# Second part of the down projection by seven products, residual additions of three norms by accumulating transfers, and another root and other additions for the last 256 tokens

## Chip, core and metric

The kernel runs on one core of one Trainium2 chip. The metric is the device time of one execution in microseconds (us), as the median of the runs shown; lower is better. TensorE is written PE, VectorE DVE, ScalarE ACT, GpSimd POOL, and SP is the engine whose queue issues most transfers.

## The reference, cut to what matters

One layer on 2048 tokens of 1024 channels in float32. What matters here is its end:

```
x = x + rmsnorm(merged @ w_o, norm_mix_post)        # called x1 below
h = rmsnorm(x, norm_mlp_pre)
f = square(relu(h @ w_up)) @ w_down                 # w_up 1024 x 4096, w_down 4096 x 1024
x = x + rmsnorm(f, norm_mlp_post)
rmsnorm(x, g) = x * rsqrt(mean(x * x) + 1e-6) * g
```

## The kernel before

**Layout.** Channels lie on the 128 partitions and tokens along the free axis. There are two blocks of tokens (`b` = 0, 1) of 1024, each of two halves (`t` = 0, 1) of 512. A tile is 128 x 1024: two rows of 128 channels for 512 tokens. Each operand of a product is split into a high part rounded to fp32r (by ACT, `wh` and `big`) and the rest (by DVE, `wl`, `tr`, `big`); three of the four cross products are formed. One `product` is two halves of twelve matmuls, 24 matmuls of 128x128 by 128x512, all recorded at L268 (`matmuls`).

**Down.** `w_down` is cut into four slabs `s` of 1024 rows. Within a slab the product is done as seven products `i` = 1 to 7 in place of eight (Winograd's scheme over two channel groups and the two halves `t`), for both blocks `b` and both output groups `o`, and summed over the slabs in PSUM. Products 1 and 2 both go into the output cells of `t` = 0 with `o` (tile `c00`); 5, 6, 3, 7 go into the others, and 4 into cells `u`.

**First part of down.** Product 1 is itself done by seven products in place of eight, over the grid of `o`, of two groups of slabs, and of `b` (`LEVEL`, `level_weights`, `level_weight`, `level_loads`, `level_parts`, `level_product`). Sums and differences of weights are formed by `level_weights` while up runs and are kept in DRAM (`level`); those of the tokens are formed by the sinks of `mlp_up`.

**The rest of down.** `jobs` lists products 5, 6, 3, 7 (`SHARED`), for each slab and each `b`, with one weight for both blocks; then 4 and 2 (`ALONE`) for `b` = 0 and after that for `b` = 1. `down_product` runs two products (one for each `o`) for a job. `token_cells` loads and splits the tokens of a job two jobs ahead, `weight_down` the weights, and `last_product` adds the sums up in `c00`, `c01`, `c11`, `u`. The last four jobs (`END`: product 2, `b` = 1) run for `o` = 0 only; their `o` = 1 is done by `at_end`.

**The norms.** `Finish` is the last norm of one `b` and `t`. `steps` squares the four tiles, sums them over the channels on PE (`root_pe`, L563), takes the inverse root on DVE (`root_dve`, 14 small instructions with the split), spreads it to all partitions on PE (L662), and multiplies. `finish` then adds x1, which `fetch` loaded into four more tiles, on DVE, and stores the result from SP's queue. Three of the four norms run this way as background work in `Lane` objects: each call of `bg()`, one for each product, takes a number of steps of each lane. The fourth, of `b` = 1 and `t` = 0, is split: `first_squares` prepares three tiles, and `at_end` does the fourth tile in two halves of 256 tokens. In `at_end` the sums of squares are at L1902, matmuls on ones that only fill time at L574 (`IDLE` = 7 and 9 of them), the roots at L603 to L610, the spreads at L654, and the multiplications and additions of `times` and `plus` at L124 and L118. At the end come four pairs of a multiplication and an addition on DVE, each with a store of 256 KB.

**What sets the order.** Each engine runs its own list in order. The lists come from a scheduler that takes instructions by priority; `tc.high_priority(offset)` moves work ahead, `behind()` and `ordered` tie background work to the main line, and `InOrder` keeps the traced order in `at_end`. A tile's reuse waits for whoever used its buffer before; the pool `big` has 28 buffers, `tr` 9, `fo` 6, `wh` and `wl` 3 each. `load` issues on SP's queue, `store` on ACT's, `aside` on POOL's.

Of the kernel before, what the change touches and what calls it, by code (L numbers as in the profile page):

```python
# [59 lines left out]
IDLE = (7, 9)  # L60
# [7 lines left out]
def block_kernel(  # L68
# [560 lines left out]

    def spread_dve(y, tmp):  # L630

        n = y.shape[1]
        yh, yl = small("sp", n, F32R), small("sq", n, F32R)
        nc.vector.tensor_copy(yh, y)
        sub(yl, y, f32(yh))
        if tmp is None:
            return yh, yl
        dg = mk(*tmp, F32R)
        for i, part in enumerate((yh, yl)):
            nc.vector.tensor_tensor(  # L640
                dg[:, i * T : (i + 1) * T].rearrange("p (g q) -> p g q", g=G),
                f32(ident).unsqueeze(1).to_broadcast([P, G, P]),
                f32(part).unsqueeze(2).to_broadcast([P, G, P]),
                op=ALU.mult,
            )
        return dg

# [506 lines left out]
    q2 = {}  # L1154
# [220 lines left out]
    def mlp_scale(b, buf):  # L1375

        st = None
        for t in (0, 1):
            sq = Squares(buf)
            for c in range(0, CPS, 2):  # L1380
                x = [mk(*buf) for _ in (0, 1)]
                for i in (0, 1):
                    load(x[i], x1d[b, c + i, t])
                yield 2
                sq.add(x[0], own=True)
                sq.add(x[1], own=True)
# [12 lines left out]
        yield  # L1399
# [266 lines left out]
    lanes.append(conv1)  # L1666
    def faster():
        conv1.rate = 2.8
# [13 lines left out]
    SHARED, ALONE = (5, 6, 3, 7), (4, 2)  # L1682
# [86 lines left out]
    def last_product(i, o, b, ps):  # L1769
# [14 lines left out]
        elif i == 6:  # L1784
            u[k], c01[k] = mk(*BIG), mk(*BIG)
            to(u[k], c00[k])
            mark(add(c01[k], u[k], c11[k]))
        elif i == 3:
            to(c01[k], c01[k])
            fin[b, 1].ready[o] = c01[k]  # L1790
        elif i == 7:
            to(u[k], u[k])
            mark(add(c11[k], c11[k], u[k]))
            fin[b, 1].ready[o + 2] = c11[k]
        elif i == 4:
            to(u[k], u[k])
            fin[b, 0].ready[o + 2] = u[k]
        else:
            to(c00[k], c00[k])
            fin[b, 0].ready[o] = c00[k]  # L1800

    class Finish:


        def __init__(self, b, t):
            self.b, self.t, self.x, self.ready = b, t, {}, {}
            self.order = (0, 1, 2, 3) if t else (2, 3, 0, 1)
# [6 lines left out]
        def finish(self, c):  # L1814
            y, x = self.ready[c], self.x[c]
            mul(two(y), two(y), per_token(self.rb))
            i = add(x, x, y)
            load(out[self.b, c, self.t], x)
            return i

# [5 lines left out]
        def steps(self, lag):  # L1826
            sq = Squares(FO)
            for c in self.order:
                while c not in self.ready:
                    yield 1  # L1830
                self.squares(sq, c)
                yield
            ss = sq.total()
            yield 2
# [6 lines left out]
            for c in self.order:  # L1841
                self.finish(c)
                yield

# [15 lines left out]
    def at_end(f, w, cells):  # L1860
# [3 lines left out]
        y = c00[k]  # L1864
# [46 lines left out]
        def root(h, st):  # L1911
            q = q2[f.b, f.t][:, h * HG : (h + 1) * HG]
            return spread_dve(root_dve(st[:, :HG], q), None)
# [10 lines left out]
        with tc.high_priority(offset=URGENT):  # L1924
# [5 lines left out]
            st = root_psum()  # L1930
            sums(0, before(0) + [sq[:, 0], sq[:, 1]], st, True, True)
            dg = root(0, st)
            slab(1, 1)
            rbs[0] = spread_pe(dg)
# [9 lines left out]
            st = root_psum()  # L1944
            sums(1, before(1), st, True, False)
# [4 lines left out]
            dg = root(1, st)  # L1950
            rbs[1] = spread_pe(dg)
            for n in f.order:
                times(1, n)
                plus(1, n)
# [28 lines left out]
    level = {}  # L1983

    def level_weights():

        for n in (0, 1):
            def get(s, o):
                t = fo()
                load(t, w_down[2 * s + o, 0])  # L1990
                return t

            def kept_as(k, t):
                level[k, n] = dram("level")
                aside(level[k, n], t)

            a21, a22 = get(n, 1), get(n + 2, 1)
            yield 1
            a11 = get(n, 0)
            add(a22, a21, a22)  # L2000
            kept_as(5, a22)
            yield 1
            sub(a21, a11, a21)
            kept_as(7, a21)
            yield
            sub(a11, a22, a11)
            kept_as(6, a11)
            a12 = get(n + 2, 0)
            yield 1
            sub(a12, a12, a11)  # L2010
            kept_as(3, a12)
            yield

    def level_weight(p, n):

        with tc.high_priority(offset=AHEAD):
            t = mk(p_wr, "wr")
            o = {1: 2 * n, 2: 2 * (n + 2), 4: 2 * (n + 2) + 1}.get(p)
            load(t, level[p, n] if o is None else w_down[o, 0])
            return split_w(t)  # L2020

    def level_loads(p, home):

        b, at, k = {
            1: (0, 0, (0, 0)), 2: (0, SLABS, (0, 0)), 3: (1, SLABS, (0, 0)),
            5: (1, 0, "T1"), 6: (1, SLABS, "T2"), 7: (1, SLABS, "T3"), 4: (1, SLABS, "T4"),
        }[p]
        with tc.high_priority(offset=AHEAD):
            los = [mk(*home, F32R) for _ in range(SLABS)]
            for u, lo in enumerate(los):  # L2030
                load(f32(lo), fd[b, u + at, k])
        return los

# [31 lines left out]

    cells = {}
# [13 lines left out]
    then(lambda: lanes.extend([Lane(1, chain_of(level_weights(), scales()))]), octs[1], 1)  # L2080
    got = []
    then(lambda: got.append(level_loads(LEVEL[0], BIG)), octs[-1], 5)
    then(lambda: got.append(level_loads(LEVEL[1], BIG)), octs[-1], 3)
# [4 lines left out]
    w = [level_weight(LEVEL[0], k) for k in (0, 1)]  # L2088
    here, coming = coming[0], coming[1:]
    for n, p in enumerate(LEVEL):  # L2090
        with behind():
            if n + 1 < len(LEVEL):
                following = [level_weight(LEVEL[n + 1], k) for k in (0, 1)]
# [3 lines left out]
            if n + 2 < len(LEVEL):  # L2097
                coming.append(level_loads(LEVEL[n + 2], (BIG, TR, BIG, TR, BIG)[n]))
# [4 lines left out]
    for n, (s, i, b) in enumerate(jobs[:-SLABS]):  # L2103
        if (s, i, b) == (1, 3, 0):
# [4 lines left out]
        if (s, i) == (0, ALONE[0]):  # L2109
            if b == 0:  # L2110
                lanes += [Lane(2, fin[0, 1].steps(2), fin[1, 1].steps(2))]
            else:
                lanes += [Lane(2, fin[0, 0].steps(2)), Lane(2, fin[1, 0].first_squares())]
        if n and (i in ALONE or b == 0 or (s, i) == FILL[:2]):
            w = [weight_down(i, s, o) for o in (0, 1)]
        cells = coming.pop(0)
        while len(coming) < 2 and n + 1 + len(coming) < len(jobs):
            job = jobs[n + 1 + len(coming)]
            with behind() if n < 8 else nullcontext():
                coming.append(token_cells(*job, BIG if n < 4 else TR))  # L2120
        down_product(s, i, b, w, cells)
    end = []
    for n, (s, i, b) in enumerate(END):
# [80 lines left out]
```

## Time and profile before

| | us |
|---|---|
| median of 3 runs (2167.44 to 2172.89) | 2168.49 |
| profiled execution | 2169.2 |
| its span, first to last instruction | 2167.4 |
| PE busy | 2146.1 |
| DVE busy | 1666.4 |
| ACT busy | 1036.4 |
| POOL busy | 32.3 |

A line of the timeline gives start, duration, engine, line of the kernel, operation, output and inputs by tile name, shape and count; in brackets stands the idle time before it and what ended it. A line of the windows gives the busy time of PE, weight loads, DVE, ACT and POOL in a stretch, the granted PE clock, and the transfers' share and GB/s. Durations overlap where an engine is pipelined; the spacing of starts is what an instruction takes.

### The profile page before, as it was taken

The numbers are of one execution on the slowest core, as the hardware profiler recorded it, in microseconds if no ns is written. First come the engines' busy times: TensorE is split into PE (matmuls) and PEld (weight loads), VectorE is DVE, ScalarE is ACT, GpSimd is POOL, SyncE is SP. The second block draws the span as 40 slices with busy tenths as digits, with TensorE's granted clock in tenths as the row PEclk, the third lists the DMA queues.
The fourth block names the chain that finished last, engine by engine and source line by source line (L and its number), as shares of the span: only waits on it lengthen the run. The fifth ranks groups of instructions, "written<-read, shape, count | busy, mean of one in ns | idle before, by whom it ended". The sixth has DMA issues, their size and how long they took to land.

```text
span 2167.4 us, 25192 instructions
## 1 busy us (share of the span) xinstructions
PE 2146.1 (99%) x9630; PEld 1778.2 (82%) x9630; DVE 1666.4 (77%) x1640; ACT 1036.4 (48%) x1083; POOL 32.3 (1%) x69
## 2 busy tenths in 40 slices
PE   9999999999999999999999999999999999999998
PEld 7888888888888878888888878888888888888887
DVE  8897789998688998987758785777776656546786
ACT  6444454334543535545644674655653332334551
POOL 1000000000000000000000000000000000000000
PEclk9999999999999999999999999999999999999999
DMA  7688997778997787445777698677788996555882
GB/s 276 238 300 311 325 348 279 262 251 294 336 373 252 251 318 278 181 146 194 266 288 279 241 361 320 237 258 272 298 352 305 372 341 232 174 193 186 276 300 86
DMA packets 165416, 587.97 MB, mean 271 GB/s; under 512 B 18352, under 2 KB 20656, under 8 KB 165296
## 3 DMA queue, kind: packets, MB, share of 16 engines
q1 hardware_dynamic: 145168, 513.91, 66.0%
q10 hardware_dynamic: 12672, 46.14, 5.5%
q0 software_dynamic: 7456, 26.31, 3.1%
q8 instruction: 75, 1.23, 0.2%
q14 instruction: 45, 0.37, 0.0%
HBM read 389.07 MB, written 197.23 MB: 271 GB/s over the span
## 4 chain that ended last, share of the span: by engine, by line
PE 92%; DVE 3%; DMA 2%; ACT 1%; issue 1%; SPq 0%; DVEq 0%; ACTq 0%
PE up L268 28%; PE down L268 24%; PE wo L268 7%; PE ga L268 7%; PE glu L268 5%; PE gb L268 5%; PE B L268 4%; PE rb L268 4%; PE A L268 4%; PE pool L268 3%; DVE big L121 1%; DMA tr<-yd 1%; DMA wl<-kept 1%; PE rb L563 1%; PE mix L268 1%
## 5 line engine op out<-in xcount | busy, mean ns | idle before, releaser
L268 PE MATMUL up<-big,wh 128*128 128x512 f32 x1792 | 480.9, 390 | 2.1 <-DVE big L121 1.8
L268 PEld LDWEIGHTS up<-big,wh 128*128 128x128 f32 x1792 | 335.9, 188 | 73.8 <-DVE big L121 2.9
L225 ACT CAST wh<-wr 128x1024 fp32r<-128x1024 f32 x199 | 209.0, 1051 | 375.1 <-PE up L268 91.1
L939 DVE SCALAR_TENSOR_TENSOR y<-v,cst,y 128x1024 f32<-128x1024 f32 x240 | 307.5, 1281 | 2.8
L268 PE MATMUL down<-big,wh 128*128 128x512 f32 x856 | 296.4, 390 | 0.0
L268 PE MATMUL up<-big,wl 128*128 128x512 f32 x896 | 276.2, 389 | 0.0
L225 ACT CAST wh<-ws 128x1024 fp32r<-128x1024 f32 x128 | 134.5, 1052 | 253.6 <-PE up L268 63.6
L268 PE MATMUL down<-big,wl 128*128 128x512 f32 x704 | 216.9, 389 | 0.0
L268 PE MATMUL down<-tr,wh 128*128 128x512 f32 x552 | 214.9, 389 | 0.0
L268 PEld LDWEIGHTS up<-big,wl 128*128 128x128 f32 x896 | 168.2, 188 | 34.8
L121 DVE TENSOR_TENSOR wl<-ws,wh 128x1024 fp32r<-128x1024 f32 x120 | 146.5, 1222 | 64.8 <-ACT wh L225 63.4
L268 PEld LDWEIGHTS down<-big,wh 128*128 128x128 f32 x856 | 160.7, 188 | 33.4
L121 DVE TENSOR_TENSOR wl<-wr,wh 128x1024 fp32r<-128x1024 f32 x122 | 148.7, 1220 | 45.8 <-ACT wh L225 44.7
L121 DVE TENSOR_TENSOR tr<-tr,big 128x1024 fp32r<-128x1024 f32 x92 | 110.5, 1222 | 73.8 <-ACT big L1748 64.2
L268 PEld LDWEIGHTS down<-big,wl 128*128 128x128 f32 x704 | 132.2, 188 | 27.4
L1748 ACT CAST big<-tr 128x1024 fp32r<-128x1024 f32 x82 | 84.4, 1050 | 112.2 <-DMA tr<-fd 96.2
L121 DVE TENSOR_TENSOR big<-big,big 128x1024 fp32r<-128x1024 f32 (+1 forms) x90 | 108.0, 1221 | 30.3 <-ACT big L1748 11.8
L268 PE MATMUL wo<-big,wh 128*128 128x512 f32 x480 | 128.6, 390 | 0.4 <-ACT tr L1312 0.4
L268 PE MATMUL glu<-big,wh 128*128 128x512 f32 x464 | 125.2, 391 | 1.3 <-ACT wh L225 0.9
L268 PEld LDWEIGHTS down<-tr,wh 128*128 128x128 f32 x552 | 103.6, 188 | 21.4
L268 PE MATMUL gb<-big,wh 128*128 128x512 f32 x448 | 120.0, 390 | 0.0
L268 PE MATMUL ga<-big,wh 128*128 128x512 f32 x448 | 119.9, 389 | 0.0
(212 smaller groups left out, 3356.3 us busy)
## 6 DMA issues: line engine op xcount, KB each, us to landing
tr<-fd SPq DMA_DIRECT2D x96, 512.0 KB, 5.3
wr<-w_down SPq DMA_DIRECT2D x90, 512.0 KB, 5.8
wl<-kept SPq DMA_DIRECT2D x85, 512.0 KB, 5.0
kept<-wl SPq DMA_DIRECT2D x72, 512.0 KB, 5.9
wr<-w_up SPq DMA_DIRECT2D x64, 512.0 KB, 4.8
wr<-w_in SPq DMA_DIRECT2D x60, 512.0 KB, 5.4
fd<-tr ACTq DMA_DIRECT2D x54, 512.0 KB, 3.8
fd<-tr SPq DMA_DIRECT2D x46, 512.0 KB, 3.1
```

The source lines that it names most:

```text
L121: return nc.vector.tensor_tensor(o, a, b, op=ALU.subtract)
L225: nc.scalar.copy(hi[:, :n], src[:, :n])
L268: i = nc.tensor.matmul(ps, w[wp][:, (at + k) * P : (at + k + 1) * P], rhs[k][xp], start=start and n == 0, stop=stop and n == len(order) - ...
L563: nc.tensor.matmul(st[:, at + g : at + g + 1], ss[:, g * P : (g + 1) * P], inv_n, start=start is None or (start and g == 0), stop=stop, sk ...
L939: nc.vector.scalar_tensor_tensor(acc, v[:, k : k + TB], wk, acc, op0=ALU.mult, op1=ALU.add)
L1748: nc.scalar.copy(hi, t)
```

## The change

1. **Product 2 by seven products.** `ALONE` becomes `(4,)`. Product 2 runs as `HALVES`, seven products of two halves (48 matmuls each), for both blocks at once, after `SHARED` and before product 4. The first half's weights' sums (`level_weights(2, 0)`) are formed during up of block 0, the second's during products 3 and 7. The new `level_cells` forms the sums of the tokens (16 loads, 16 subtractions, 16 stores) there too. Each `level_half` adds its sum into `c00` on DVE.
2. **Three norms.** `Finish.steps` no longer loads x1: POOL issues a transfer that adds x1 to the scaled tile, and after four of these four stores. The norms of `t` = 1 start with the halves, that of `b` = 0, `t` = 0 with product 4.
3. **The last 256 tokens.** `root_short` takes eight small instructions; the block's epsilon times its factor (`floors`) is added to the sum of squares by a matmul, and the root is spread in plain float32 without a split (`spread_whole`). `IDLE` becomes (7, 5). Two of the four last additions go to POOL; the other two read products written to PSUM, and the very last store is halved over two queues.

The diff, cut to its core:

```diff
-IDLE = (7, 9)
+IDLE = (7, 5)
...
+    def root_short(a, scale):
...
+        y = sm("sy", I32)
+        nc.vector.tensor_scalar(y, a.bitcast(I32), -0.5, MAGIC, op0=ALU.mult, op1=ALU.add)
+        y = f32(y)
+        h = sm("s1")
+        mul(h, y, y)
+        h2 = sm("s2")
+        mul(h2, h, a)
+        h = step(ALU.add, h2, -10.0 / 3.0, h2, "s1")
+        y = step(ALU.add, h, 5.0, y, "sy")
+        h = sm("s1")
+        mul(h, y, y)
+        h = step(ALU.mult, h, -0.5 * 0.375**3 * scale, a, "s2")
+        return step(ALU.add, h, 1.5 * 0.375 * scale, y, "sy")
...
+    def spread_whole(y):
+
+        rb = mk(ps_rb, "rb", F32, (P, T))
+        for g in range(y.shape[1]):
+            nc.tensor.matmul(
+                rb[:, g * P : (g + 1) * P], y[:, g : g + 1].to_broadcast([P, P]), f32(ident),
+                start=g == 0, stop=True, skip_group_check=True,
+            )
+        return rb
...
+        if b:
+            f = floors[b] = p_const.tile([P, G], F32, tag="floor", name="floor")
+            nc.vector.tensor_scalar(
+                f, st[:, :G], EPS, EPS**0.5 * SQ, op0=ALU.add, op1=ALU.mult
+            )
+            mul(f, f, f)
...
+    lanes.append(Lane(1, when_idle(level_weights(2, 0, window, lambda: mk(p_y, "y")), 42)))
...
-    SHARED, ALONE = (5, 6, 3, 7), (4, 2)
+    SHARED, ALONE = (5, 6, 3, 7), (4,)
...
             dg = spread_dve(root_dve(st, q2[self.b, self.t]), FO)
-            self.fetch(self.order)
             yield lag
             self.rb = spread_pe(dg)
             yield 1
             for c in self.order:
-                self.finish(c)
+                y = self.ready[c]
+                mul(two(y), two(y), per_token(self.rb))
+                nc.gpsimd.dma_start(y, x1d[self.b, c, self.t], accum_op=ALU.add)
                 yield
+            for c in self.order:
+                aside(out[self.b, c, self.t], self.ready[c])
+            yield
...
+            rbs[1] = spread_whole(root(st))
+            for n in f.order[:2]:
+                times(1, n)
+                x = at(f.x[n], 1)
+                nc.gpsimd.tensor_tensor(x, x, at(f.ready[n], 1), op=ALU.add)
+                load(two(out[f.b, n, f.t])[:, :, HT:], x)
+            scaled = {}
+            for k, n in enumerate(f.order[2:]):
+                scaled[n] = ps[:, k * T : (k + 1) * T].rearrange("p (c t) -> p c t", c=2)
+                mul(
+                    scaled[n], at(f.ready[n], 1),
+                    rbs[1][:, :HT].unsqueeze(1).to_broadcast([P, 2, HT]),
+                )
+            n = f.order[2]
+            x = at(f.x[n], 1)
+            add(x, x, scaled[n])
+            load(two(out[f.b, n, f.t])[:, :, HT:], x)
+            for i, queue in enumerate((store, load)):
+                x = at(f.x[c], 1)[:, i]
+                add(x, x, scaled[c][:, i])
+                queue(two(out[f.b, c, f.t])[:, i, HT:], x)
...
+                if k == 22:
+                    t = mk(*(BIG if u % 2 else FO))
+                    sub(t, here[22], here[12])
+                    kept_as("V3", u + SLABS, t)
+                elif k == 12:
+                    sub(here[12], here[12], here[11])
+                    kept_as("V1", u, here[12])
+                elif k == 11:
+                    sub(here[22], here[22], here[12])
+                    kept_as("V2", u + SLABS, here[22])
+                else:
+                    sub(here[21], here[21], here[22])
+                    kept_as("V4", u + SLABS, here[21])
...
+    def level_half(p, n, w, cells):
+
+        a = {1: "x", 2: "z", 6: "x", 7: "x", 4: "x", 5: "y", 3: "y"}[p]
+        if p in (1, 2, 5) and n == 0:
+            sums_of[a] = psum("down")
+        ps = sums_of[a]
+        product(
+            ps, w, cells, start=p in (1, 2, 5) and n == 0, stop=p in (2, 4, 3) and n == 1
+        )
+        if n:
+            k = {1: (0, 0), 2: (0, 0), 6: (0, 1), 3: (0, 1), 5: (1, 1), 7: (1, 1), 4: (1, 0)}[p]
+            with tc.high_priority(offset=AHEAD):
+                mark(add(c00[k], c00[k], ps))
+            if p in (2, 3, 7, 4):
+                fin[k[1], 0].ready[k[0]] = c00[k]
+        bg()
...
+    HALVES = [(p, n) for p in LEVEL for n in (0, 1)]
+    at = next(n for n, job in enumerate(jobs) if job[1] in ALONE)
+    PREPARE = (0, 3, 0)
+    items = jobs[:at] + HALVES + jobs[at:]
...
+        if item == PREPARE:
+            lanes.append(Lane(1.2, chain_of(level_weights(2, 1, fo), level_cells())))
+        if (s, i, b) == (0, ALONE[0], 0):
+            lanes.append(Lane(3, fin[0, 0].steps(2, 150)))
```

In the code after the change, weights and cells of a half are prepared two halves ahead, and the loads of its cells four ahead.

More of the change, by code (lines that the diff above doesn't have):

```diff
@@ L1812, in fetch @@
                 load(self.x[c], x1d[self.b, c, self.t])
[L1814 to L1819, printed above, removed]
         def squares(self, sq, c):
@@ L1909, in before, with floor, root @@
             return [f.ss[:, h * HT : (h + 1) * HT]]
-        def root(h, st):
-            q = q2[f.b, f.t][:, h * HG : (h + 1) * HG]
-            return spread_dve(root_dve(st[:, :HG], q), None)
+        def floor(h):
+            st = root_psum()
+            nc.tensor.matmul(
+                st[:, :HG], f32(ident), floors[f.b][:, h * HG : (h + 1) * HG],
+                start=True, stop=False, skip_group_check=True,
+            )
+            return st
+        def root(st):
+            return root_short(st[:, :HG], SQ)
         def times(h, c):
@@ L1943, in at_end @@
             plus(0, c)
-            st = root_psum()
-            sums(1, before(1), st, True, False)
+            st = floor(1)
+            sums(1, before(1), st, False, False)
             idle(IDLE[0], first[:, :T])
@@ L1982, in block_kernel, with level_weight @@
     LEVEL = ORDER
[L1983 to L2014, printed above, removed]
+    def level_weight(part, p, n):
         with tc.high_priority(offset=AHEAD):
```

182 lines of the change are left out of this document (137 added, 45 removed).

## The prediction

> **What bounds the kernel now.** I read the page first (busy shares, then the chain that ended last), then the waits of PE, then windows by stage from the end back, then the timeline of the last 80 us. A window starts where a stage's first matmul is, counted back from the end.
>
> ```profile
> PE 2146.1 (99%) x9630; PEld 1778.2 (82%) x9630; DVE 1666.4 (77%) x1640; ACT 1036.4 (48%) x1083; POOL 32.3 (1%) x69
> ...
> PE 92%; DVE 3%; DMA 2%; ACT 1%; issue 1%; SPq 0%; DVEq 0%; ACTq 0%
> ```
>
> PE is busy for 2146 of 2167 us and makes 92% of the chain. A matmul taken away anywhere before the end shortens the run, as long as PE is still fed; the few us in which PE is idle lie in the tail.
>
> ```profile
> core 0: us, PE busy (x) PEld busy (x) DVE busy (x) ACT busy (x) POOL busy (x), PEclk, DMA share, GB/s
> ...
> 1558.00:1636.00 78.00, 78.00 (x346) 64.58 (x345) 57.75 (x50) 43.85 (x45) 0.00 (x0) 1.00 0.85 332
> 1636.00:1723.00 87.00, 87.00 (x385) 72.09 (x384) 54.51 (x47) 31.57 (x32) 2.12 (x4) 1.00 0.94 351
> ...
> 1810.00:1897.00 87.00, 87.00 (x386) 72.06 (x385) 48.76 (x43) 30.61 (x32) 0.00 (x0) 1.00 0.56 193
> 1897.00:1973.00 76.00, 76.00 (x337) 62.96 (x336) 39.77 (x35) 26.73 (x28) 0.00 (x0) 1.00 0.52 178
> ...
> 2104.00:2126.00 22.00, 22.00 (x99) 18.23 (x98) 21.60 (x19) 13.90 (x15) 0.00 (x0) 1.00 0.42 149
> ```
>
> These are the first part of down by seven products (1558), products 5 (1636), 3 (1810) and 7 (1897), and the four END jobs (2104). PE is full in each, also where transfers run at 351 GB/s, and where DVE is busy for 98% of a stretch. So a stage of either kind is not lost by its mean load; it is lost where one input comes late.
>
> **Part 1, the matmuls.** Product 2 was 4 slabs x 2 blocks x 2 outputs = 16 products of 24 matmuls, 384. It becomes 14 halves of 24, 336. The instruction lists of both programs agree: 2368 full matmuls into `down` and its `rb` banks before, 2320 after.
>
> ```profile
> 2094.23 0.84 PE L268 MATMUL down<-big,wl 128*128 128x512 f32 x3
> ...
> 2096.95 0.84 PE L268 MATMUL down<-big,wl 128*128 128x512 f32 x3
> ```
>
> Twelve matmuls lie between these two starts: 2.72 / 12 = 0.2267 us. 48 x 0.2267 = **-10.9 us**, if PE stays fed.
>
> **Its price on DVE.** The lists show 25 more DVE instructions of 128x1024: 16 in `level_cells`, 8 in the second `level_weights`, 12 more splits of cells, 3 more joins; 2 fewer splits of weights and 12 fewer additions of x1.
>
> ```profile
> 2083.23 4.62 DVE L121 TENSOR_TENSOR tr<-tr,big 128x1024 fp32r<-128x1024 f32 x4
> ...
> 2095.07 0.15 DVE L610 SCALAR_TENSOR_TENSOR s<-s 128x4 f32<-128x4 f32 x1
> 2095.26 0.16 DVE L610 SCALAR_TENSOR_TENSOR sy<-s,sy 128x4 f32<-128x4 f32 x1
> ...
> 2096.53 0.68 DVE L640 TENSOR_TENSOR fo<-ident,sp 128x512 fp32r<-128x512 f32 x1
> 2097.13 0.69 DVE L640 TENSOR_TENSOR fo<-ident,sq 128x512 fp32r<-128x512 f32 x1
> ```
>
> Back to back, 128x1024 takes (4.62 - 1.22) / 3 = 1.13 us, 128x512 0.60, a small one 0.20. Products 3 and 7 (163 us, DVE 88.5) get 20 of the new ones, 23 us: 68% busy, hidden behind PE. Their 40 new transfers of 512 KB are 21 MB, 129 GB/s on top of 193 and 178; the stage at 351 shows room for that. Four more run during up of block 0, where the new list puts them after the convolution's work; they too cost nothing. If that cover is gone, each costs 1.1 us.
>
> The halves are the tight place. They last 14 x 24 x 0.2267 = 76.2 us, and the new DVE list holds, from the join before them up to the join that ends them, 58 instructions of 128x1024, 5 of 128x512 and 14 small: 65.5 + 3.0 + 2.8 = 71.3 us, 94%. I walked the list against PE's. It is on time except in two places. In the second half of sub-product 2, a cell's split ends 0.5 us after PE wants it. Then PE wants the spread of the norm of `b` = 0, `t` = 1 eight matmuls into the second half of sub-product 7, 7.3 us after sub-product 5 ends; but DVE has to do the join of sub-product 5, three splits, the last twelve small instructions and the two 128x512 of the spread in between: 4 x 1.13 + 12 x 0.20 + 2 x 0.60 = 8.1, and some 0.3 of handing over: 1.1 us late. With ragged edges I take **+2.0**, from 0 (all handed over early) to 10 (first rival). What waits behind a late split is the whole PE list, so each such wait counts in full.
>
> **Part 2, the norms.** The 12 additions of x1 leave DVE; the multiplications stay. Nothing on PE's path waits for a stored tile except buffers: casts for `at_end`'s weights wait for the stores of the norm `b` = 1, `t` = 1, scaled some 35 us before.
>
> ```profile
> fd<-fo POOLq DMA_DIRECT2D x22, 512.0 KB, 6.6
> big<-x1d SPq DMA_DIRECT2D x16, 512.0 KB, 7.0
> out<-big SPq DMA_DIRECT2D x12, 512.0 KB, 6.0
> ...
> x1d<-big POOLq DMA_DIRECT2D x8, 512.0 KB, 5.6
> ```
>
> No row shows an accumulating transfer. Below it costs a plain one, 5.6; above, a load and a store one after the other, 7.0 + 6.0 = 13.0. I take 8, near the plain rows, then a 6 us store: 14 of the 35. The last norm (`b` = 0, `t` = 0) is scaled while `at_end` runs, and here POOL's two last additions are queued behind its four stores, which wait for its accumulations. Its last multiplication ends about 6.5 us after the first join of `at_end` and POOL's first addition is due about 20 us after that join, so an accumulation has 13 us before it delays anything. Cost at 8: nothing. The Trainium skill, "Collectives: The Full Stack", section "The bandwidth ceiling: the fold count and why AG ≠ RS ≠ AR", speaks against this: an add in the transfer needs two reads, so it runs at about half a copy's rate. By that 6.6 becomes about 13, an estimate, and the slack would be just used up; no run here shows it yet.
>
> ```profile
> 2098.31 0.62 PE L662 MATMUL rb<-fo,ones 128*128 128x512 f32 x2
> ...
> 2138.41 0.39 PE L268 MATMUL down<-big,big 128*128 128x256 f32 x1 [0.78 <-DVE big L118]
> ```
>
> One small gain: PE's list puts this norm's spread (two matmuls, 0.45) into the 0.78 us that PE idles at `at_end`'s first join: **-0.4**.
>
> **Part 3, the tail.**
>
> ```profile
> 2152.01 0.69 DVE L118 TENSOR_TENSOR big<-big,down 128x512 f32<-128x512 f32 x1 [1.15 <-PE down L268]
> 2152.17 1.87 PE L574 MATMUL rb<-ones 128*128 128x512 f32 x7
> ...
> 2154.86 0.16 DVE L124 TENSOR_TENSOR s<-rb,q 128x2 f32<-128x2 f32 x1 [1.56 <-PE rb L1902]
> ...
> 2157.54 0.30 PE L654 MATMUL rb<-ident,sp 128*128 128x128 f32 x1 [0.55 <-DVE sp L634]
> ...
> 2158.24 0.69 DVE L124 TENSOR_TENSOR big<-big,rb 128x512 f32<-128x512 f32 x1 [0.64 <-PE rb L654]
> ...
> 2162.93 0.69 DVE L118 TENSOR_TENSOR big<-big,big 128x512 f32<-128x512 f32 x1
> ```
>
> From the first root instruction to PE's spread are 2.68 us; eight small ones and 0.15 of handing over make 1.75: -0.9. The floor's matmul ahead of the sums adds 0.1. The spread has two float32 matmuls for four in fp32r; before it takes 0.70 (2157.54 to 2158.24), and I take 0.7, from 0.4 (half) to 1.4 (double). DVE's eight instructions spaced 0.67 (2158.24 to 2162.93 is seven) last 5.4 to 2163.6. Now there are four multiplications and one addition of 128x512, 3.35, and two of 128x256, about 0.4 each: 4.15, so -1.2. Four fewer fillers: nothing, they end before the root.
>
> ```profile
> 2.21 0.30 POOL L725 CAST ident<-tr 128x128 fp32r<-128x128 f32 x1
> ...
> 2159.68 4.51 SPq L127 DMA_DIRECT2D out<-big  x4
> ...
> out<-big SPq DMA_DIRECT2D x8, 256.0 KB, 2.4
> ```
>
> POOL's two additions hide if each takes under 1.7. Bounds: 0.69 as on DVE; 2.4, eight times the cast's 0.30 (four times its width, two inputs). I take 1.4; at 2.4 the end is 1.4 later. The Trainium skill, "GPSIMD Engine Reference", section "3.1 Elementwise — side-by-side cycle accounting", has such an addition at 1.96 times DVE's, 1.35 by our row: hidden as well. The last store has half the bytes: from 0 to -0.6, I take -0.2. Tail: -0.9 + 0.1 - 1.2 - 0.2 = **-2.2**.
>
> **Sum.** 2169.2 - 10.9 + 2.0 - 0.4 - 2.2 = 2157.7 against the profiled execution. That one lies 0.7 above the median of 2168.49, so **2157** as a median.
>
> **Rivals.** *PE waits at handovers in the halves.* For it: the cast and the split of a cell follow each other on two engines, each in order.
>
> ```profile
> L121 DVE TENSOR_TENSOR big<-big,big 128x1024 fp32r<-128x1024 f32 (+1 forms) x22 | 26.0, 1220 | 10.3 <-ACT big L1074 8.1 <-ACT big L1748 2.2
> ...
> L121 DVE TENSOR_TENSOR tr<-tr,big 128x1024 fp32r<-128x1024 f32 x8 | 9.4, 1220 | 4.0 <-ACT big L1074 4.0
> ...
> L121 DVE TENSOR_TENSOR tr<-tr,big 128x1024 fp32r<-128x1024 f32 x92 | 110.5, 1222 | 73.8 <-ACT big L1748 64.2 <-PE down L268 5.1 <-ACT big L1074 4.0
> ```
>
> In the first part of down, DVE idles 14.3 us before 30 splits, 0.48 each. With 28 splits that is 13.4 in the halves, where only 4.9 are free: PE is 8.5 late in place of 2.0, **2163.5**. Against it: there PE never waited, so DVE was early; and in the halves casts come two halves ahead. *The same on the slower side:* over the whole kernel the wait is 73.8 / 92 = 0.80 for a split. At that, for 42 splits of cells and weights, 33.6 - 4.9 = 28.7 us late: **2184**. It decides from (4.9 + 2 + 11.5) / 42 = 0.44 us per split of all 42 for no gain, and 0.6 for slower by over 0.3%.
>
> *Accumulations hold up the tail.* Place: POOL's additions behind the four stores. Beyond 13 us each us counts; at 20 us it is **2164**. Against it: the plain rows.
>
> That the change doesn't take the matmuls away is excluded by the lists.
>
> **How the numbers follow.** About 0.3% (6.5 us) is what a measurement can tell from no change: faster is below 2162.0, slower above 2175.0. Forecast (2153 to 2161): 0.62. First rival at 2161 to 2168: 0.18; its slower form: 0.08. Accumulations late, 2158 to 2172: 0.09, half of it below 2162. Better than 2153: 0.03. Faster: 0.62 + 0.03 + 0.05 + 0.05 of the first rival's edge = 0.75; slower 0.08; same 0.17. The range begins at 2153 (no wait, -2.0; the best ends of the spread and the store, -0.3 and -0.4; and 1 us, by which the fastest run of before lies under its median) and ends at 2166, past the first rival.
>
> **What would show it.** In the changed profile: 48 fewer L268 matmuls into `down`; PE's busy share of the halves (76 us before product 4) near full, with waits of 1 to 3 us on a DVE split or the spread; the landing of the accumulating transfers under 13 us; the last root in eight instructions; DVE's last addition some 9.5 us after the last join's start, 11.6 before. Wrong would be PE idle for over 5 us in the halves, or POOL's additions starting late.

## The result, and the profile after

| | before | after |
|---|---|---|
| median of 12 runs, run in turns | 2171.03 | 2163.52 |
| lowest and highest | 2166.32, 2172.89 | 2161.95, 2173.23 |
| ratio of after to before, 95% interval | | 0.9978 (0.9969 to 0.9987) |
| profiled execution | 2169.2 | 2163.6 |
| its span | 2167.4 | 2161.7 |

By the ratio of the runs the change makes the kernel faster by 0.22% (0.13 to 0.31), some 5 us; the medians lie 7.5 us apart, the means 4.6 (2170.2 and 2165.5). That is below the 0.3% that the prediction called measurable; the twelve runs in turns resolve a little more. The forecast of 11.5 us was more than twice the gain by the ratio. 2163.5 lies inside the range of 2153 to 2166, near the first rival's 2163.5, but not by that rival's mechanism: that is luck. Six of the twelve runs of the changed kernel had a mean granted clock of 0.997 or 0.998 and took 2162.0 to 2163.4 us, the other six 0.994 or 0.995 and 2163.6 to 2173.2; the profiled one, at 0.995, is of the second kind, so the slow clock that its trace shows below need not be in every run.

The page of the changed kernel, the lines that answer to those of before:

```profile
PE 2139.8 (99%) x9582; PEld 1772.0 (82%) x9582; DVE 1688.4 (78%) x1654; ACT 1044.3 (48%) x1093; POOL 78.0 (4%) x143
...
PE 88%; DVE 5%; DMA 4%; issue 1%; ACT 1%; SPq 0%; DVEq 0%; ACTq 0%
```

PE has its 48 matmuls fewer, but is busy for 6.3 us less, not 10.9, and its share of the chain fell from 92% to 88%. DVE and transfers took the difference: somewhere PE waited. All waits of PE after 1900 us (engine, line, tile waited for; sum, times, longest):

```profile
PE rb L563 <- DVE fo L118: 2.4, 1, 2.4
PE down L268 <- DVE tr L121: 0.5, 1, 0.5
PE rb L678 <- DVE sy L639: 0.4, 1, 0.4
PE down L268 <- DVE big L118: 0.3, 1, 0.3
PE rb L698 <- DVE fo L666: 0.2, 1, 0.2
```

The two that were predicted are there: 0.5 at a split in sub-product 2 and 0.2 at the spread (1.1 predicted). The largest was not predicted: 2.4 us at the sum of squares of the norm `b` = 1, `t` = 1. PE asks for it at 2063, in product 4, 15 us behind the end of the halves (they run from 1969 to 2048). Windows of the changed kernel around it:

```profile
2020.00:2040.00 20.00, 19.79 (x88) 16.03 (x87) 19.10 (x24) 17.30 (x22) 4.69 (x6) 1.00 1.01 316
2040.00:2060.00 20.00, 20.00 (x90) 16.57 (x89) 17.31 (x16) 15.48 (x18) 1.12 (x2) 1.00 0.95 346
2060.00:2080.00 20.00, 17.57 (x68) 14.22 (x67) 15.32 (x28) 5.25 (x5) 0.89 (x1) 0.83 0.51 183
```

Two things show. The transfers' share stands at 1.01 while only 316 GB/s move (before, 351 GB/s went at 0.94). And behind the wait the granted clock is 0.83 for 20 us, which is full speed lost for 3.4 us. The timeline of PE shows the same, first the wait, then matmuls 0.43 apart (0.85 for two, from 2068.24 to 2069.09) in place of 0.227:

```profile
2065.71 1.67 PE L563 MATMUL rb<-inv_d,fo 128*128 128x1 f32 x8 [2.43 <-DVE fo L118]
...
2068.24 0.63 PE L268 MATMUL down<-big,wh 128*128 128x512 f32 x1
2068.66 0.63 PE L268 MATMUL down<-tr,wh 128*128 128x512 f32 x1
2069.09 0.63 PE L268 MATMUL down<-big,wl 128*128 128x512 f32 x1
```

So 2.4 + 3.4 = 5.8 us went in one place. A row of ACT and rows of DVE say what the sum (DVE's last row, at 2064.96) waited for; the transfers issued from 2020 to 2055 stand below them (count, KB each, median us from issue to landing). The cells (`tr<-fd`) are tokens of product 4, loaded while the halves end.

```profile
2050.53 1.05 ACT L1827 CAST big<-tr 128x1024 fp32r<-128x1024 f32 x1 [3.07 <-DMA tr<-fd]
```

```profile
2051.61 1.23 DVE L121 TENSOR_TENSOR tr<-tr,big 128x1024 fp32r<-128x1024 f32 x1 [1.13 <-ACT big L1827]
...
2055.12 1.23 DVE L121 TENSOR_TENSOR tr<-tr,big 128x1024 fp32r<-128x1024 f32 x1 [1.14 <-ACT big L1827]
...
2057.90 1.23 DVE L121 TENSOR_TENSOR wl<-wr,wh 128x1024 fp32r<-128x1024 f32 x1 [0.43 <-ACT wh L225]
...
2064.96 0.69 DVE L118 TENSOR_TENSOR fo<-fo 128x512 f32<-128x512 f32 x1
```

```profile
q1 hardware_dynamic: 2167, 7.91, 58.6%
q0 software_dynamic: 1045, 3.82, 43.3%
...
tr<-fd SPq DMA_DIRECT2D x6, 512.0 KB, 11.9
big<-x1d POOLq DMA_DIRECT2D x4, 512.0 KB, 9.9
out<-big POOLq DMA_DIRECT2D x4, 512.0 KB, 7.6
```

Cells land 11.9 us after their issue while the four accumulating transfers of the norm `b` = 0, `t` = 1 run; a cast on ACT waits 3.07 us for one, DVE 1.13 and 1.14 for the casts and 0.43 for a cast of weights behind them, 2.70 in all, and the sum that stands behind these in DVE's list comes late. POOL's queue (q0) takes 43.3% of the 16 engines for 3.82 MB, SP's (q1) 58.6% for 7.91 MB.

**A measure for the rest.** Up to the first matmul of down's first level the two kernels run nearly the same list, but in the profiles of this study that matmul starts anywhere from 1554.3 to 1563.8 us: much of the noise of whole runs is made before it. So each profile is read from that matmul to the end of the span, the *stretch*: before 2167.4 - 1556.0 = 611.4, after 2161.7 - 1555.55 = 606.2, so -5.2 against a forecast of -11.5. There is one profile for each kernel; the five below that have neither a wait nor a slow clock at this sum or in product 5 (e2, e8, e9, e10, e11) give 600.2 to 600.7.

### The profile page after: what moved, and what is told of

Read it like the earlier page. It is cut to its first block, busy times and chain, and to the rows that moved or that the text cites. A ratio compares the mean times of both kernels' runs of the same rounds, so it can differ in the third digit from the quotient of the medians.

```text
span 2161.7 us, 25309 instructions
## 1 busy us (share of the span) xinstructions
PE 2139.8 (99%) x9582; PEld 1772.0 (82%) x9582; DVE 1688.4 (78%) x1654; ACT 1044.3 (48%) x1093; POOL 78.0 (4%) x143
## 4 chain that ended last, share of the span: by engine, by line
PE 88%; DVE 5%; DMA 4%; issue 1%; ACT 1%; SPq 0%; DVEq 0%; ACTq 0%
PE up L268 26%; PE down L268 22%; PE wo L268 8%; PE ga L268 7%; PE gb L268 5%; PE glu L268 5%; PE rb L268 4%; PE B L268 4%; PE A L268 4%; PE pool L268 3%; DVE y L975 1%; DMA big<-xt 1%; DVE big L121 1%; DMA tr<-yd 1%; DMA wl<-kept 1%
## 5 line engine op out<-in xcount | busy, mean ns | idle before, releaser
L268 PE MATMUL down<-tr,wh 128*128 128x512 f32 x504 | 197.2, 391 | 0.5 <-DVE tr L121 0.5
L121 DVE TENSOR_TENSOR big<-big,big 128x1024 fp32r<-128x1024 f32 (+1 forms) x108 | 129.4, 1219 | 32.2 <-ACT big L1110 12.3
L1827 ACT CAST big<-tr 128x1024 fp32r<-128x1024 f32 x70 | 72.0, 1049 | 102.9 <-DMA tr<-fd 79.6
L268 PEld LDWEIGHTS down<-tr,wh 128*128 128x128 f32 x504 | 95.2, 189 | 20.9 <-DVE tr L121 1.1
```

Of the source, the lines that this page charges most:

```text
L121: return nc.vector.tensor_tensor(o, a, b, op=ALU.subtract)
L268: i = nc.tensor.matmul(ps, w[wp][:, (at + k) * P : (at + k + 1) * P], rhs[k][xp], start=start and n == 0, stop=stop and n == len(order) - ...
L1827: nc.scalar.copy(hi, t)
```

## The experiments

**Theory:** an accumulating transfer keeps the DMA engines busy about twice as long per byte as a plain one; cells land late, DVE comes late to one sum, and PE's wait there costs clock as well. **Rivals:** the bytes alone crowd the queues, added or not; DVE's list alone makes the sum late; and, for the tail, transfers beside it eat its gain. Medians below are beside before's 2170.4 to 2171.3 of the same chip (2168.5 for e11).

**e1, plain transfers into other tiles.**

```diff
-                nc.gpsimd.dma_start(y, x1d[self.b, c, self.t], accum_op=ALU.add)
+                if (self.b, self.t) == (0, 1):
+                    nc.gpsimd.dma_start(mk(*BIG), x1d[self.b, c, self.t])
+                else:
+                    nc.gpsimd.dma_start(y, x1d[self.b, c, self.t], accum_op=ALU.add)
```

> The four transfers of the norm b=0, t=1 that add x1 into the scaled tile become plain transfers of the same 512 KB of x1, from the same place in POOL's list, into tiles that nobody reads (so x1 is left out of this quarter of the output). PE's list is unchanged. Theory 1 (an accumulating transfer keeps the 16 DMA engines busy about twice as long per byte as a plain one, so the cells of the halves land late): the cells land in 6 to 8 us between 2020 and 2055 in place of 11.9, PE's wait of 2.43 us at the sum of squares of the norm b=1, t=1 (L563) is gone or below 0.5, and the time is 2157 to 2159. Rival (the bytes alone crowd the queues, whether they are added or not): cells still land in over 10 us, the wait stays between 2 and 3 us, 2163. Rival (DVE's list alone makes that sum late): the wait stays, 2163.

Measured: 2164.38, ratio 0.9969 (0.9955 to 0.9982), stretch 604.7. The wait stayed and the cells still took 11.4 us to land, which speaks for the bytes; the 1.5 us less than the changed kernel are a shorter slow stretch (clock 0.91 from 2060 to 2080, so 1.8 us lost). PE's row, then SP's first issue of a pair of cells in e1 and in the changed kernel:

```profile
2064.52 1.05 PE L563 MATMUL rb<-inv_d,fo 128*128 128x1 f32 x8 [2.49 <-DVE fo L118]
```

```profile
2017.80 0.32 SPq L127 DMA_DIRECT2D big<-fd  x1
```

```profile
2013.58 0.32 SPq L127 DMA_DIRECT2D big<-fd  x1
```

Counted from the first matmul of the stretch, SP issues this cell at 463.5 in e1 and at 458.0 in the changed kernel, 5.5 us later: the four extra `big` tiles hold up loads into `big`. POOL issues the x1 transfers earlier as well, the first at 2012.74 in place of 2025.05. So e1 changed more than the addition, and is no test of it. e9 is. What e1 does show is that cells can land as late with no addition at all; that loads held back and then issued together crowd the queues there is argued, not shown.

**e2, the four accumulating transfers left out.**

```diff
-                nc.gpsimd.dma_start(y, x1d[self.b, c, self.t], accum_op=ALU.add)
+                if (self.b, self.t) != (0, 1):
+                    nc.gpsimd.dma_start(y, x1d[self.b, c, self.t], accum_op=ALU.add)
```

> The four accumulating transfers of the norm b=0, t=1 are left out (x1 is left out of this quarter of the output); its stores stay. Theory 1 and the rival of the bytes: cells land in 6 to 7 us, no wait at the sum of the norm b=1, t=1, 2157 to 2158. Rival of DVE's list (nothing in it changes): the wait of 2.4 us stays, 2163.

Measured: 2162.80, ratio 0.9960 (0.9946 to 0.9974), stretch 600.6. The cells land in 6.3 us and the wait is gone. The median missed the expectation, the stretch met it (in this profile the stretch begins at 1558.97, 3.4 us later than in the changed kernel's). DVE's list alone is not the cause, but how near it is to the edge shows here: DVE's last instruction of the sum, then PE's first on it.

```profile
2065.68 0.69 DVE L118 TENSOR_TENSOR fo<-fo 128x512 f32<-128x512 f32 x1
```

```profile
2066.53 0.95 PE L563 MATMUL rb<-inv_d,fo 128*128 128x1 f32 x8
```

A DVE instruction of this shape back to back takes 0.60, so the sum is there at 2066.3 and PE takes it at 2066.53. With no disturbance at all the slack is 0.2 us at most (in the changed kernel PE starts 0.15 us after the sum is there).

**e3, the sum asked for later.**

```diff
-            yield 2 if sooner else 3
+            yield 2 if sooner else 3 if self.b == 0 else 7
```

> All transfers stay; the norm b=1, t=1 asks for its sum of squares on PE 70 matmuls (16 us) later. All theories: PE no longer waits 2.43 us there. If the wait also costs clock afterwards (matmuls spaced 0.43 for some 6 us, as seen behind it), the gain is 2.4 + 3.6 = 6 us: 2157.5. If the slow stretch comes from something else in that place, only 2.4 us: 2161. If DVE is behind by more than the sum shows, the wait moves to a split of a cell: 2163.

Measured: 2160.29, ratio 0.9944 (0.9928 to 0.9960), stretch 601.4, of which 1.1 went at a wait of 0.8 and its refilling in product 5, long before the place of the edit. PE runs from 2060 to 2080 at clock 1.00. The gain is 4.8 us of the stretch, with that wait 5.9: what the wait and the slow clock had cost.

**e4, part 2 undone.**

```diff
+            self.fetch(self.order)
             yield lag
...
-                nc.gpsimd.dma_start(y, x1d[self.b, c, self.t], accum_op=ALU.add)
+                x = self.x[c]
+                add(x, x, y)
+                load(out[self.b, c, self.t], x)
...
-            for c in self.order:
-                aside(out[self.b, c, self.t], self.ready[c])
...
```

> Part 2 undone alone: all three final norms load x1 by SP, DVE adds it and SP stores, as before the change (12 more additions of 128x1024 on DVE); the seven products in halves and the new tail stay. Theory 1: without accumulating transfers the cells land in 6 to 8 us, and the eight additions that fall among the halves and product 4 cost PE 0 to 2 us in waits; tail 0.7 better: 2157 to 2160. Rival of DVE's list: DVE was at 94% in the halves, and four more additions (4.5 us) ahead of the next sums make them later than before: 2166 to 2169. Rival of the bytes: the same bytes, the same late landing, 2163.

Measured: 2180.34, ratio 1.0043 (1.0027 to 1.0059), stretch 619.1: slower than before, and further than any theory said. PE's largest waits after 1900, and SP's issues around the first:

```profile
PE down L268 <- ACT big L1110: 5.4, 1, 5.4
PE down L268 <- ACT big L225: 4.7, 1, 4.7
PE down L268 <- DVE tr L121: 2.0, 2, 1.5
```

```profile
2015.00 0.32 SPq L127 DMA_DIRECT2D wr<-level  x1
2033.68 1.23 SPq L127 DMA_DIRECT2D big<-fd  x2
```

For 18 us SP issues nothing, and the next that it issues is a pair of cells into `big`, the tiles of which the x1 loads now hold four until DVE has added and SP itself has stored. Whether it is these tiles or DVE's twelve additions was not taken apart. What the run shows: part 2, priced at nothing, is worth 13 us beside the halves (619.1 against 606.2). Half clock for 10.2 and for 6.8 us is part of the 619.1; the changed kernel has one spell of 6.8.

**e5, the wait filled with matmuls.**

```diff
-            add(o, o, self.ss[:, T:])
+            self.whole = add(o, o, self.ss[:, T:]).ins
...
+            if (self.b, self.t) == (1, 1):
+                idle(10, root_psum(), sq.whole)
             st = root_pe(ss, inv_n=inv_d)
```

`sq.whole` only places the ten matmuls in the list, next to the sum.

> The changed kernel with ten matmuls of 128x512 on constants (2.27 us at 0.227) put on PE right ahead of the sum of squares of the norm b=1, t=1, where PE waited 2.43 us. They add no work to the path as long as that wait is there. If the wait is what halves the clock behind it (6.8 us at half speed in the changed kernel's profile, 3.4 in that of the plain transfers), the profile shows full clock after 2060 and some 0.2 to 0.5 us of idle time, and the stretch from the first matmul of down's first level to the end is 606.2 - 3.4 = 602.8 us. If the slow stretch has another cause, it stays, and the stretch is 606. The median would be some 2 us below that of the changed kernel, by which only the profile decides.

Measured: 2161.92, ratio 0.9964 (0.9952 to 0.9976), stretch 604.2, 2.0 less than the changed kernel. The window and PE's row:

```profile
2060.00:2080.00 20.00, 19.18 (x88) 15.64 (x87) 16.89 (x28) 7.18 (x7) 0.89 (x1) 1.00 0.56 193
```

```profile
2067.81 1.05 PE L563 MATMUL rb<-inv_d,fo 128*128 128x1 f32 x8 [0.81 <-DVE fo L118]
```

The clock is full although ten useless matmuls were added, which speaks for the wait as what halved it. The stretch missed its 602.8 by 1.4: 0.81 us of waiting is left in place of 0.2 to 0.5, and from the fillers' start to the next full matmul PE takes 4.2 us, where in e9 the sum alone takes 0.8. These 3.4 us on top of e9's 600.7 give 604.1.

**e6, the sum 4 matmuls later.**

```diff
-            yield 2 if sooner else 3
+            yield 2 if sooner else 3 if self.b == 0 else 4
```

> The changed kernel with the norm b=1, t=1 asking for its sum only 4 matmuls (0.9 us) later. The wait should be 2.43 - 0.9 = 1.5 us. If every wait of that size halves the clock for at least one interval of 3.4 us (the waits of 1.4 to 1.9 us at 759 did in four of five profiles), 1.7 us go on top, and the stretch from down's first level to the end is 606.2 - 3.4 + 1.7 - 0.9 = 603.6; without a slow stretch 601.9. If the transfers move along with the sum, the wait stays at 2.4.

Measured: 2162.45, ratio 0.9964 (0.9951 to 0.9976), stretch 601.9.

```profile
2066.53 1.05 PE L563 MATMUL rb<-inv_d,fo 128*128 128x1 f32 x8 [1.16 <-DVE fo L118]
```

The wait of 1.16 left the clock at 1.00 behind it (window 2060 to 2080). Of the profiles of the changed kernel and its variants (e4 apart), the two with a wait of 2.43 and 2.49 us at this sum (the changed kernel and e1) have half clock behind it, and the eight with 1.16 or less do not. Four matmuls, 0.9 us, are worth 4.3.

**e7, part 3 alone on the kernel before.** The edit is the change's part 3, nothing else.

> The kernel before with part 3 alone (shorter root, spread in two float32 matmuls, POOL's two additions, halved last stores). No norm transfers run beside the tail here. From the end of at_end's first join (2138.4 in before) to the end of the span it took 29.0 us; predicted is 29.0 - 2.2 = 26.8. If the tail edit is worth less by itself, 27.5, as in the changed kernel (29.0 before against 27.8 there, from the same point). The median then falls by 1 to 2 us, below what the rounds can tell.

Measured: 2168.23, ratio 0.9989 (0.9980 to 0.9998), stretch 610.4. From the first matmul behind `at_end`'s first join to the end of the span it is 2165.8 - 2138.0 = 27.8; before 2167.4 - 2138.4 = 29.0; after 2161.7 - 2134.0 = 27.8. The tail edit is worth 1.2, with transfers beside it and without.

**e8, late sum, and the last norm's accumulating transfers left out.**

```diff
-                nc.gpsimd.dma_start(y, x1d[self.b, c, self.t], accum_op=ALU.add)
+                if (self.b, self.t) != (0, 0):
+                    nc.gpsimd.dma_start(y, x1d[self.b, c, self.t], accum_op=ALU.add)
```

> The late sum of e3 again, with the four accumulating transfers of the last norm (b=0, t=0) left out (x1 is left out of that quarter of the output); its stores stay. If these transfers cost the tail the 0.7 us that the changed kernel's tail fell short of the forecast, the last stores of 256 KB land in 2.4 to 4 us in place of 8.3 and from the end of at_end's first join to the end it is 27.1 in place of 27.8. If the stores were late for nothing that counts, 27.8 as before. The median is that of e3, 2160, either way, and together they say how firm the gain of the late sum is.

Measured: 2162.98, ratio 0.9957 (0.9945 to 0.9970), stretch 600.3. The tail is 2161.2 - 2133.5 = 27.7, though from 2130 on SP's stores of 256 KB land in 2.4 us in place of 8.3. These transfers cost the tail nothing; and the late sum's stretch is again 6 us under the changed kernel's.

**e9, plain transfers in place.** Here no instruction moves and no tile is added.

```diff
-                nc.gpsimd.dma_start(y, x1d[self.b, c, self.t], accum_op=ALU.add)
+                if (self.b, self.t) == (0, 1):
+                    nc.gpsimd.dma_start(y, x1d[self.b, c, self.t])
+                else:
+                    nc.gpsimd.dma_start(y, x1d[self.b, c, self.t], accum_op=ALU.add)
```

> The changed kernel with every instruction in its place; only the four transfers of the norm b=0, t=1 write x1 over the scaled tile in place of adding it (the scaled values are left out of that quarter of the output). Same tiles, same waits, same bytes, plain transfers. In e1 the plain transfers went to other tiles and left earlier, so it did not settle whether adding costs more. If the addition inside the transfer is what makes the cells late: landing of these four 5 to 7 us in place of 9.9, of the cells 6 to 8 in place of 11.9, the wait at the sum of the norm b=1, t=1 below 1 us, the stretch from down's first level to the end 601 to 602 us. If the bytes are: cells at 9 to 12, wait 2 to 2.5, stretch 604 to 606.

Measured: 2158.64, ratio 0.9941 (0.9925 to 0.9957), stretch 600.7. The transfers of 2020 to 2055 and PE's row:

```profile
q1 hardware_dynamic: 2474, 8.98, 65.6%
q0 software_dynamic: 1152, 4.19, 31.3%
...
tr<-fd SPq DMA_DIRECT2D x6, 512.0 KB, 8.1
big<-x1d POOLq DMA_DIRECT2D x4, 512.0 KB, 5.8
```

```profile
2065.01 0.95 PE L563 MATMUL rb<-inv_d,fo 128*128 128x1 f32 x8
```

Same bytes, same places, and the wait is gone. POOL's queue takes 31.3% for 4.19 MB (7.5% per MB) where it took 43.3% for 3.82 MB (11.3% per MB) with half of it accumulating; if the stores take 7.5, the accumulating half takes about 15, an estimate, twice as long. SP's plain transfers took 7.4% per MB beside the additions and 7.3% here, so plain bytes kept their price. DVE waits 0.18 us ahead of the sum where it had waited 2.70, and the sum starts 2.65 us earlier, counted from the first matmul of the stretch. For this kernel that settles it for the theory, on one profile of each: the addition, not the bytes.

**e10, late sum and the last stores on other queues.**

```diff
-            load(two(out[f.b, n, f.t])[:, :, HT:], x)
-            for i, queue in enumerate((store, load)):
+            store(two(out[f.b, n, f.t])[:, :, HT:], x)
+            for i, queue in enumerate((load, store)):
```

> The late sum of e3, and in the tail the store of the third tile goes to ACT's queue, the first half of the last tile to SP's and the second half to ACT's (before: SP, ACT, SP), so that no queue has to issue three stores within 1.3 us. In the changed kernel the last half is added at 2157.3 and SP issues its store only at 2157.86, after two others of 0.53 to 0.62 us each. Expected: the last issue within 0.1 us of the last addition, 0.5 us gained, from the end of at_end's first join to the end 27.3 us in place of 27.8; the stretch from down's first level 599.8, the median 2159 to 2160. If the end is set by something else, 27.8.

Measured: 2158.73, ratio 0.9938 (0.9922 to 0.9954), stretch 600.3. A miss for its own edit: the last store is issued 0.14 us after the last addition in place of 0.56, and the tail is 2157.5 - 2129.7 = 27.8 as in the changed kernel. A window of the changed kernel, then one of before, suggest why:

```profile
2158.00:2158.50 0.50, 0.00 (x0) 0.00 (x0) 0.00 (x0) 0.00 (x0) 0.00 (x0) 0.50 1.02 336
```

```profile
2164.50:2165.00 0.50, 0.00 (x0) 0.00 (x0) 0.00 (x0) 0.00 (x0) 0.00 (x0) 0.50 0.25 90
```

With quicker additions 768 KB of stores leave within 1.3 us, and the DMA engines are full from 2158 to 2160 (shares of 0.97 to 1.02); in e10 they are as full from 2153.5 to 2155.5 (0.93 to 1.01), whichever queue goes first. In before they were not: 0.60, 0.25, 0.99 and 0.25 from 2164 to 2166.

**e11, e10 with five fillers in place of seven.**

```diff
-IDLE = (7, 5)
+IDLE = (5, 5)
```

> e10 with five filler matmuls in place of seven between the old sums and the last squares in the tail. In the changed kernel these seven start 0.38 us after the second join (0.16 in before, ahead of the floor's matmul), end at 2149.85, and the sums of the last squares start then, though ACT has both squares at 2149.2. If the fillers are what makes the first root instruction come 3.07 us after the join (2.85 before), two fewer bring it to 2.65, and from the end of at_end's first join to the end it is 27.3 us in place of 27.8. If PE's clock falls without them or the squares are later than they look, 27.7 to 28. The median is that of e10, 2158 to 2159, within what the rounds can tell.

Measured: 2159.98, ratio 0.9960 (0.9945 to 0.9974), stretch 600.15. The tail is 2157.7 - 2130.4 = 27.3, as expected. The start of the second join and of the first root instruction:

```profile
2144.17 0.69 DVE L118 TENSOR_TENSOR big<-big,down 128x512 f32<-128x512 f32 x1 [1.09 <-PE down L268]
...
2146.78 0.16 DVE L643 TENSOR_SCALAR sy<-rb 128x2 int32<-128x2 int32 x1 [1.33 <-PE rb L1977]
```

2.61 us in place of 3.07: fillers had stood in front of the last sums. The medians of e10 and e11 don't tell them apart. e3, e10 and e11 compute the whole output, as e5 and e6 do, and are the fastest kernels that do so: 2160.29, 2158.73 and 2159.98. The intervals of e3 and e10 lie below the changed kernel's, that of e11 overlaps with it; by the stretch all three are 4.8 to 6 us under it.

## Why the prediction failed, point by point

**The matmuls: right.** 48 x 0.2267 = 10.9. From 1969 to 2047.6, the halves, PE is busy for 77.9 of 78.6 us, as foreseen, and DVE for 70.4 (71.3 foreseen). (The stages of before begin up to 4 us earlier than the windows of the prediction, down's first level at 1556.0 and not 1558; nothing in the sum hangs on that.)

**The handovers in halves: right in kind, smaller.** +2.0 was taken; the waits were 0.5 and 0.2, and with the pipeline's refilling around each they cost some 1.3 (0.8 and 0.5). The first rival, a wait at every split, did not happen.

**The failed step: "Cost at 8: nothing".** In part 2 I priced the accumulating transfers by their own landing alone (8 us taken, 9.9 measured here, inside 5.6 to 13.0) and asked only who waits for their tiles: nobody on PE's path does. What they do to the loads beside them was not in the sum. Four of them run while the halves end, beside the loads of product 4's cells, and these take 11.9 us in place of 8.1 (e9 against the changed kernel). So DVE waits 2.70 us for casts, its sum for the norm `b` = 1, `t` = 1 comes 2.65 us later than in e9, and PE waits 2.43 for it. The walk that found DVE "on time except in two places" could not see this: it held the lists side by side only up to the join that ends the halves, at 2048, and it names no cell that lands late. This third place lies 15 us behind, with a slack of 0.2 us at most (e2, e9). The room at 351 GB/s was claimed for the new transfers in products 3 and 7; for the transfers beside the halves the sum had no term.

**A term was missing: the clock.** A wait of 2.43 us cost another 3.4 us behind it, in the profiled run. e5 (filled: full clock) and e6 (1.16 us: full clock) show that the wait set it off; e1 shows that much the same wait can cost 1.8. In the sum each us of waiting counted as one us.

**Ledger of the stretch.** -10.9 (matmuls) + 1.3 (the two predicted waits) + 5.8 (the wait and its clock; e9, without them, is 5.5 shorter) - 0.45 (the spread hidden in the join's gap, now 0.33 in place of 0.78, as foreseen) - 1.2 (tail) = -5.45, measured -5.2. What the 0.25 left over is was not traced. Without the 5.8 the sum says -11.25; e8, e9 and e10 measure -11.1, -10.7 and -11.1. That the forecast's -11.5 comes so near to these is in part luck: the handovers cost 0.7 less than was taken and the tail gave 1.0 less.

**The tail: 1.2 in place of 2.2.** In the changed kernel the second join, the first root instruction, the first multiplication and the last additions are:

```profile
2147.77 0.69 DVE L118 TENSOR_TENSOR big<-big,down 128x512 f32<-128x512 f32 x1 [1.09 <-PE down L268]
...
2150.84 0.16 DVE L643 TENSOR_SCALAR sy<-rb 128x2 int32<-128x2 int32 x1 [1.78 <-PE rb L1977]
...
2153.22 1.28 DVE L124 TENSOR_TENSOR big<-big,rb 128x512 f32<-128x512 f32 x2 [0.87 <-PE rb L678]
...
2155.95 1.35 DVE L118 TENSOR_TENSOR big<-big,down 128x512 f32<-128x512 f32 x3
```

Root to first multiplication is 2.38 (3.38 before): -1.0, foreseen -0.9. Multiplications and additions end 4.1 later (5.4 before): -1.3, foreseen -1.2. The last addition ends 9.5 after the join, as foreseen, and POOL's two additions take 2.49 us together (1.4 each taken) and hide. But the floor's matmul costs 0.2 before each root in place of 0.1 in all; in the second it pushes seven fillers ahead of the last sums (e11), and the last store was put at -0.2 and is +0.6: the end comes 4.4 after the last addition, 3.8 before, as stores that were 1.3 us apart now run together (e10).

**Part 2 in the tail: right.** Twelve accumulating transfers land in 8.8 us at the median and POOL's additions start as their data come; the second rival suspected the right transfers, but in another stage and by another path, POOL's own queue in place of the loads beside them.

**The pages.** The Trainium skill, "Collectives: The Full Stack", section "The bandwidth ceiling: the fold count and why AG ≠ RS ≠ AR", has the reduce of a collective's ring, an add that needs two reads, at half a copy's rate. The engines' share agrees (about 15% against 7.5% per MB), the landing less so (9.9 against 5.8). I weighed that rule for the transfer's own landing, where it changed nothing, and not for the engines that it shares with others. The skill's "TensorE: Matmul & The Clock Gate", section "Why this matters for your kernels", warns of idle gaps over some 3 us; here a gap of 2.43 was enough (eight matmuls of one column, 0.8 us, follow it), at 760 us one of 1.4, and the measurement decides.

## What to carry to other kernels

Ask of every new transfer not only who waits for it, but which loads run beside it: here an accumulating transfer took the DMA engines about twice as long per byte, and what felt it was the place with no slack. Follow the lists past the end of the stage that was changed: the wait came 15 us behind it. A background result that PE picks up needs slack of its own, and asking for it a few matmuls later cost nothing: 0.9 us later was worth 4 us here. And when a "same bytes" experiment is made, it must keep tiles and order as well, or it tests them (e1 against e9).

## What the hardware showed that was not expected

Up to PE's last matmuls the clock is halved for 3.4 us or a multiple of it (3.4, 6.8 and once 10.2 us in the traces' clock record), and a wait below that length can set it off, but not always. At 760 us every kernel here has one wait of 1.4 to 2.2 us before a sum (of eight matmuls of one column, some 0.9 us); in 11 of 13 profiles the window from 755 to 775 shows a clock of 0.91 or 0.83 (20 us x 0.09 or 0.17: 1.8 or 3.4 us lost), in two 1.00. A row of each of three kernels, before, e9 and e8:

```profile
755.00:775.00 20.00, 18.20 (x78) 14.79 (x77) 16.44 (x24) 3.48 (x5) 0.53 (x1) 0.91 0.87 329
```

```profile
755.00:775.00 20.00, 18.55 (x86) 15.03 (x86) 18.37 (x26) 3.88 (x5) 0.53 (x1) 1.00 0.90 348
```

```profile
755.00:775.00 20.00, 17.79 (x69) 14.41 (x68) 14.74 (x20) 4.70 (x7) 0.53 (x1) 0.83 0.76 278
```

The longest wait, 2.2 us in e8, has the 0.83. But waits of 1.45 and 1.39 us left the clock at 1.00 in e9 and at 0.91 in e4, and waits of 1.66 and 1.71 at 1.00 in e1 and at 0.91 in e10. So the same instructions with nearly the same wait cost nothing or 1.8 us more, run by run. That goes some way to explain why whole runs scatter over 5 to 10 us, and why a change of 5 us is read more surely from the profile's stretch than from a median of five runs.
